# One more K-pair by seven products, and the evacuation of a PSUM bank as one ScalarE copy, in a four-layer transformer trunk

## The chip, the cores and the metric

The kernel runs on one core of one Trainium2 chip. The metric is the device time of one execution in microseconds, over everything the kernel does: loading the weights from HBM, all four sublayer pairs, and the store of the output. A core has TensorE (PE; its weight loads are listed apart as PEld), VectorE (DVE), ScalarE (ACT), GpSimd (POOL) and SyncE (SP), each with an instruction queue of its own, which works in order. TensorE writes to PSUM, of which the kernel uses eight banks of 512 fp32 columns.

## The reference, cut to what matters

Sequence length is 256, model width 2048, MLP width 8192, and there are four residual layers: a mixer and an MLP, twice (`DEPTH = 2`; the first mixer is latent attention with an mLSTM, the second dilated attention). The change touches the MLPs and the final norm alone:

```
def squared_relu_mlp(h, w1, w2):
    return jnp.square(jax.nn.relu(h @ w1)) @ w2

    for layer in range(DEPTH):
        i = layer // 2
        h = rms_norm(x, norm_mix[layer])
        ...
        x = x + mix
        x = x + squared_relu_mlp(rms_norm(x, norm_mlp[layer]), mlp_w1[layer], mlp_w2[layer])
    return rms_norm(x, norm_final)
```

`w1` is 2048 x 8192 and `w2` 8192 x 2048 in each of the two layers, in float32.

## The kernel before

**Three-pass products.** Every float32 operand is split in a high part in the format `FR` (float32r), in which it goes to TensorE, and the remainder (`hi`, `lo`; `xh`, `xl`). For a weight tile `wr` ScalarE writes the high part `wh` (line 135) and VectorE the remainder `wl` (line 136). A product is then three matmuls (`mm_three`, lines 154 to 156). In the first MLP product, which is made with features on the partitions, a matmul of 512 columns takes both parts of the tokens at once (line 164), and one of 256 columns adds the weight's remainder (line 168); the two halves of the PSUM bank must be added afterwards.

**The MLP.** The hidden width is worked in four quarters of 2048 features, 16 blocks of 128 each. A block `h` is 32 matmuls into one bank (bank 3 for all blocks but the first eight of a layer); its evacuation, `evac_h`, adds the two halves with `both` (lines 283 to 286): ScalarE copies the upper half of the bank to SBUF (`bt_h`), VectorE adds the lower half, still in PSUM, to it (`hu`). Then ScalarE applies Relu and Square. The next block can't start before both of these reads of the bank are done, since it writes the same bank.

**The second product** multiplies a quarter's 2048 hidden features, as eight pairs of 128-row K tiles, with `w2`, for two column ranges of 1024 one after the other ("first half" and "second half" of the quarter below). A pair is done in one of two ways. `steps_seven` does the 2 x 2 block product of a pair with seven block products rather than eight: 21 matmuls of 512 columns, in two steps of 9 (`go_a`) and 12 (`go_b`). It needs sums of weight tiles (`ta`, `tb`, lines 225 to 228), each split again in high part and remainder, and sums of the hidden tiles, made in `evac_h` (`hp`, then `pt`, lines 1039 to 1047). `eight` does it directly: 24 matmuls, two weight tiles of 128 x 1024, and hidden tiles `ht`. `SEVEN`, line 22, says how many of the eight pairs go by seven products, 5 here.

**Order.** `woven` puts the steps of the sevens between the blocks: in the first half of a quarter between its blocks 8 to 15, in the second half between blocks 0 to 7 of the next quarter. Then come the eights. After these VectorE adds the results to the residual `x` (`late_y`, line 1074; `early_y`, lines 1055 to 1065, after the sevens). The last quarter has no second half of this kind: in the first layer it has three sevens and five eights there, whatever `SEVEN` is, and in the second layer `finish` does those columns directly. The program's text is not the order on the engines: a scheduler orders each engine's queue at build time, and the rows in the section on the change show what it made.

**Buffers.** Raw weight tiles have 4 buffers, `wh` and `wl` 4 each, those of `ta` and `tb` 3 each. `hp` has two, `bt` two of 256 columns, `pt` has `SEVEN`, `ht` 2 x (8 - `SEVEN`).

Of the kernel before, what the change touches and what calls it, by code (L numbers as in the profile page):

```python
# [9 lines left out]
F32 = mybir.dt.float32  # L10
FR = mybir.dt.float32r
AF = mybir.ActivationFunctionType
OP = mybir.AluOpType

P = 128
S = 256
# [2 lines left out]
KD = D // P  # L19
FF = 8192  # L20
NQ = 4
SEVEN = 5
EPS = 1e-6
BIG = -3.0e38
MLA_SCALE = 192 ** -0.5
# [44 lines left out]
def trunk(ctx: ExitStack, tc: tile.TileContext, plan, a, c_first, c_even, c_odd, out):  # L70
    nc = tc.nc
# [23 lines left out]
    def acc(name, bank=None):  # L95

        if bank is None:
            bank = n_a[0] % 4
            n_a[0] += 1
        return pacc.tile([P, 512], F32, name=name, tag=f"acc{bank}", bufs=1)  # L100
# [181 lines left out]
    def both(pool, out, ac, name):  # L282

        t = pool.tile([P, S], F32, name=f"bt_{name}", tag="bt", bufs=2)
        nc.scalar.activation(t, ac[:, S:], AF.Copy)
        nc.vector.tensor_add(out, ac[:, :S], t)  # L286
# [664 lines left out]
    def finish(H, wq, evac_y, scale, sm):  # L951

        gfs = []
        for i in range(2):
            gfs.append(sm.tile([P, 1024], F32, name=f"gf{i}", tag="hp", bufs=2))
            nc.gpsimd.dma_start(gfs[i], a["norm_final"][i * 1024:(i + 1) * 1024]
                                .rearrange("(o d) -> o d", o=1).to_broadcast([P, 1024]))

        def gf(lo, hi):
            return gfs[lo // 1024][:, lo % 1024:(hi - 1) % 1024 + 1]  # L960

        ss = [sm.tile([P, 5], F32, name=f"ss_f{b}") for b in range(NB)]

        def stats(b, i, v):
            nc.scalar.activation(junk[:, :v.shape[-1]], v, AF.Square, accum_out=ss[b][:, i:i + 1])

        def gain(c):
            def go():
                for b in range(NB):
                    nc.vector.tensor_mul(x[b][c], x[b][c], gf(c * 512, (c + 1) * 512))  # L970
            return go

        for c in range(2):
            for b in range(NB):
                stats(b, c, x[b][c])
        weave(steps_tokens(Late(H), wq, 1024, 512, evac_y(2), name="y"), [gain(0), gain(1)])
        for b in range(NB):
            stats(b, 2, x[b][2])

        def add(b, o, ac):  # L980
            nc.vector.scalar_tensor_tensor(x[b][3][:, o:o + 256], ac[:, :256], scale["s"][:, b:b + 1],
                                           x[b][3][:, o:o + 256], OP.mult, OP.add)

        def evac_a(ac):
            for b in range(NB):
                add(b, 0, ac[b])
                stats(b, 3, x[b][3][:, 0:256])
                nc.vector.tensor_mul(x[b][3][:, 0:256], x[b][3][:, 0:256], gf(1536, 1792))

        weave(steps_tokens(Late(H), wq, 1536, 256, evac_a, kt=4, name="y"), [gain(2)])  # L990
        w = [weights(wq, k, 4, 1792, 256) for k in range(0, 16, 4)]
        for b in range(NB):
            ac = acc(f"z{b}")
            for k in range(16):
                hi, lo = (t[:, k % 4, :] for t in w[k // 4])
                mm_three(ac[:, :256], operand(H[k], b), (hi, lo), k == 0, k == 15)
            add(b, 256, ac)
            stats(b, 4, x[b][3][:, 256:])
            t = sm.tile([P, 3], F32, name=f"var_f{b}")
            nc.vector.tensor_reduce(t[:, 0:1], ss[b], mybir.AxisListType.X, OP.add)  # L1000
            nc.vector.tensor_scalar(t[:, 1:2], t[:, 0:1], 1.0 / D, EPS, OP.mult, OP.add)
            nc.gpsimd.tensor_tensor(t[:, 2:3], t[:, 1:2], neg_half[:, :1], OP.pow)
            r = t[:, 2:3]
            rows = slice(b * P, (b + 1) * P)
            for c in (0, 1):
                nc.vector.tensor_scalar(x[b][c], x[b][c], r, None, OP.mult)
                nc.sync.dma_start(out[0, rows, c * 512:(c + 1) * 512], x[b][c])
            nc.vector.scalar_tensor_tensor(x[b][3][:, 256:], x[b][3][:, 256:], r, gf(1792, 2048), OP.mult, OP.mult)
            nc.scalar.activation(x[b][2], x[b][2], AF.Copy, scale=r)
            nc.sync.dma_start(out[0, rows, 1024:1536], x[b][2])  # L1010
            nc.scalar.activation(x[b][3][:, 0:256], x[b][3][:, 0:256], AF.Copy, scale=r)
            nc.sync.dma_start(out[0, rows, 1536:2048], x[b][3])

    def mlp(layer, norm, nxt):
        st = ExitStack()
        sm = st.enter_context(tc.tile_pool(name=f"mlp{layer}", bufs=1))
# [4 lines left out]
        def evac_h(H):  # L1021
            def make(c):
                box = {}

                def go(f, ac):
                    u = sm.tile([P, S], F32, name="hu", tag="hu", bufs=2)
                    both(sm, u, ac, "h")
                    nc.scalar.activation(u, u, AF.Relu)  # L1028
                    if c >= SEVEN:
                        nc.scalar.activation(u, u, AF.Square)  # L1030
                        H[2 * c + f] = sm.tile([P, 2, S], FR, name="ht", tag="ht", bufs=2 * (NF // 2 - SEVEN))
                        split_to(H[2 * c + f], u)
                        return
                    if f == 0:
                        box["r"] = sm.tile([P, 8, P], F32, name="hp", tag="hp", bufs=2)
                    r = box["r"]
                    dst = r[:, 1:3, :] if f == 0 else r[:, 0:4:3, :]
                    v = u.rearrange("p (b t) -> p b t", b=NB)
                    nc.scalar.activation(dst, v, AF.Square)
                    if f == 1:  # L1040
                        nc.vector.tensor_tensor(r[:, 4:6, :], r[:, 1:3, :], r[:, 2:4, :], OP.subtract)
                        nc.vector.tensor_tensor(r[:, 6, :], r[:, 5, :], r[:, 1, :], OP.subtract)
                        nc.vector.tensor_tensor(r[:, 7, :], r[:, 0, :], r[:, 6, :], OP.add)
                        pt = sm.tile([P, 2, 8, P], FR, name="pt", tag="pt", bufs=SEVEN)
                        nc.scalar.activation(pt[:, 0], r, AF.Copy)
                        nc.vector.tensor_tensor(pt[:, 1], r, pt[:, 0].bitcast(F32), OP.subtract)
                        H[2 * c], H[2 * c + 1] = (pt, 0), (pt, 1)
                return go
            return make
# [56 lines left out]
        for q in range(NQ):  # L1106
            last = q == NQ - 1
            wq = ("mlp_w2", layer, q * (FF // NQ))
            seven, eight = steps_seven(sm, H, list(range(SEVEN)), wq, 0, early_y(0), late_y(0))
            woven(hs[NF // 2:], sum(seven, []))  # L1110
            run(*eight)
            if last and nxt is None:
                finish(H, wq, evac_y, scale, sm)
                break
            pairs = list(range(3 if last else SEVEN))
            seven, eight = steps_seven(sm, H, pairs, wq, 1024, early_y(2), late_y(2))
# [78 lines left out]
```

## Time and profile before

| | |
|---|---|
| median of 3 runs | 2154.32 us (2150.76 to 2155.19) |
| profiled execution | 2148.98 us, its span 2147.1 us |
| TensorE busy | 2116.2 us, 99% of the span |
| VectorE busy | 1667.3 us, 78% |
| ScalarE busy | 1249.1 us, 58% |
| granted TensorE clock, mean | 0.999 |
| moved by DMA | 404.51 MB, 188 GB/s |

The profiled execution is one run; 1.9 us of its time lie outside the span. A matmul's duration in the trace (about 390 ns for 512 columns) is longer than the distance to the next one's start, since matmuls overlap in the array: what TensorE can do is read from starts, and its busy share of 99% hides short stalls. Instructions on VectorE overlap a little too.

### The profile page before, as it was taken

What the parts mean: (1) busy time and instruction counts of PE and PEld (TensorE: products, weight loads), DVE (VectorE), ACT (ScalarE), POOL (GpSimd) and SP (SyncE); (2) the same over time, 40 slices, a digit from 0 to 9 for tenths busy, and PEclk for the clock granted to TensorE, in tenths of its full rate; (3) what the DMA queues carried; (4) which work ended last, traced back from release to release, by engine and by line L of the source; (5) the groups of instructions that cost most, each with busy time, mean ns of one, the idle gap of its engine ahead of it and who ended that gap; (6) DMA issues with size and microseconds to landing.
All of it is one profiled execution on the core that took longest, in us unless ns stands there. A gap on an engine that the chain in (4) does not pass through costs nothing. (4 is left out here: it accounts for less than half of the span.)

```text
span 2147.1 us, 29491 instructions
## 1 busy us (share of the span) xinstructions
PE 2116.2 (99%) x10995; PEld 1808.9 (84%) x10995; DVE 1667.3 (78%) x2346; ACT 1249.1 (58%) x1851; POOL 5.6 (0%) x12
## 2 busy tenths in 40 slices
PE   9999999999999999999999999999999999999998
PEld 8998888888888888888888888888888888888887
DVE  5678556878978888998877667557888889888975
ACT  6676445666665665666544544556656656566653
POOL 0000000000000000000000000000000000000000
PEclk9999999999999999999999999999999999999999
DMA  8554555555555555565555555455556556556664
GB/s 296 170 175 145 166 179 177 185 197 187 198 191 197 193 187 200 189 197 195 195 195 170 179 171 176 160 188 174 190 191 198 194 196 195 198 188 195 211 207 141
DMA packets 115279, 404.51 MB, mean 188 GB/s; under 512 B 12928, under 2 KB 13568, under 8 KB 115136
## 3 DMA queue, kind: packets, MB, share of 16 engines
q1 hardware_dynamic: 114624, 401.07, 56.7%
q8 instruction: 86, 1.41, 0.3%
q0 software_dynamic: 368, 1.51, 0.3%
q14 instruction: 57, 0.47, 0.1%
q10 hardware_dynamic: 144, 0.06, 0.0%
HBM read 400.49 MB, written 2.10 MB: 187 GB/s over the span
## 5 line engine op out<-in xcount | busy, mean ns | idle before, releaser
L136 DVE TENSOR_TENSOR wl<-wr,wh 128x1024 fp32r<-128x1024 f32 (+4 forms) x769 | 876.5, 1146 | 352.4 <-ACT wh L135 343.2
L135 ACT ACTIVATE wh<-wr 128x1024 fp32r<-128x1024 f32 (+4 forms) x769 | 763.2, 996 | 585.9 <-PE h L164 154.7
L164 PE MATMUL h<-T,wh 128*128 128x512 f32 x2048 | 518.1, 395 | 15.2 <-DVE hu L286 14.3
L164 PEld LDWEIGHTS h<-T,wh 128*128 128x128 f32 x2048 | 370.6, 188 | 107.4 <-DVE hu L286 37.3
L168 PEld LDWEIGHTS h<-T,wl 128*128 128x128 f32 x2048 | 279.2, 190 | 20.3
L168 PE MATMUL h<-T,wl 128*128 128x256 f32 x2048 | 285.3, 282 | 0.0
L154 PE MATMUL yc<-wh,ht 128*128 128x512 f32 x360 | 140.3, 390 | 0.0
L155 PE MATMUL yc<-wl,ht 128*128 128x512 f32 x360 | 140.2, 389 | 0.0
L156 PE MATMUL yc<-wh,ht 128*128 128x512 f32 x360 | 140.1, 389 | 0.0
L1028 ACT ACTIVATE hu<-hu 128x256 f32<-128x256 f32 x128 | 52.6, 415 | 109.8 <-DVE hu L286 109.8
L155 PE MATMUL ym<-wl,pt 128*128 128x512 f32 x292 | 114.5, 392 | 0.0
L154 PE MATMUL ym<-wh,pt 128*128 128x512 f32 x292 | 114.5, 392 | 0.0
L156 PE MATMUL ym<-wh,pt 128*128 128x512 f32 x292 | 113.6, 389 | 0.0
L225 DVE TENSOR_TENSOR ta<-wr,wr 128x1024 f32<-128x1024 f32 x73 | 89.2, 1222 | 30.6 <-DMA wr<-in_mlp_w 30.3
L154 PE MATMUL o<-wh,M 128*128 128x512 f32 x256 | 102.3, 399 | 0.0
L156 PE MATMUL o<-wh,M 128*128 128x512 f32 x256 | 99.8, 390 | 0.0
L155 PE MATMUL o<-wl,M 128*128 128x512 f32 x256 | 99.7, 389 | 0.0
L135 ACT ACTIVATE wh<-tb 128x1024 fp32r<-128x1024 f32 x73 | 76.9, 1053 | 35.5 <-DVE tb L228 35.2
L135 ACT ACTIVATE wh<-ta 128x1024 fp32r<-128x1024 f32 x73 | 77.0, 1055 | 30.4 <-DVE ta L225 30.2
L155 PE MATMUL yc<-wl,pt 128*128 128x512 f32 x235 | 91.8, 390 | 0.0
L154 PE MATMUL yc<-wh,pt 128*128 128x512 f32 x235 | 91.7, 390 | 0.0
L156 PE MATMUL yc<-wh,pt 128*128 128x512 f32 x235 | 91.6, 390 | 0.0
(314 smaller groups left out, 3343.0 us busy)
## 6 DMA issues: line engine op xcount, KB each, us to landing
wr<-in_mlp_w SPq DMA_DIRECT2D x512, 512.0 KB, 3.6
wr<-in_od_w_qkv SPq DMA_DIRECT2D x96, 512.0 KB, 4.2
wr<-in_ev_w_in SPq DMA_DIRECT2D x32, 512.0 KB, 3.5
wr<-in_ev_w_out SPq DMA_DIRECT2D x32, 512.0 KB, 3.4
wr<-in_od_w_out SPq DMA_DIRECT2D x32, 512.0 KB, 3.5
wr<-in_ev_w_in SPq DMA_DIRECT2D x24, 344.0 KB, 3.1
wr<-in_ev_w_in SPq DMA_DIRECT2D x15, 364.0 KB, 5.5
wr<-in_mla_w_ukv SPq DMA_DIRECT2D x8, 512.0 KB, 3.6
```

What stands on the lines that cost most here:

```text
L135: nc.scalar.activation(hi, raw, AF.Copy)
L136: nc.vector.tensor_tensor(lo, raw, hi.bitcast(F32), OP.subtract)
L154: nc.tensor.matmul(ac, xh, hi, start=first, stop=False)
L155: nc.tensor.matmul(ac, xh, lo, start=False, stop=False)
L156: nc.tensor.matmul(ac, xl, hi, start=False, stop=last)
L164: nc.tensor.matmul(acs[f], hi[:, j, f * P:(f + 1) * P], Ts[j].rearrange("p a t -> p (a t)"), start=first and j == 0, stop=False)
L168: nc.tensor.matmul(acs[f][:, :S], lo[:, j, f * P:(f + 1) * P], Ts[j][:, 0, :], start=False, stop=last and j == n - 1)
L225: nc.vector.tensor_tensor(ta, r0, r1[:, 0:1, :].to_broadcast([P, 2, 512]), OP.add)
L1028: nc.scalar.activation(u, u, AF.Relu)
```

## The change

`SEVEN` goes from 5 to 6, so one more pair in each half of a quarter is done by seven products; this applies to the first half of all quarters and to the second half of three quarters, in both layers. By `SEVEN`, `pt` gets six buffers and `ht` four. To make room, `hp` gets one buffer. The evacuation of a block no longer uses `both`: ScalarE copies the whole bank, 512 columns, to SBUF (now line 1027), and VectorE adds the two halves in SBUF (now line 1029). `bt` has two buffers of 512 columns. In `finish` the gains of the final norm are loaded in three pieces, into the buffers of `hp` and `bt`, not two.

```diff
-SEVEN = 5
+SEVEN = 6
...
-        for i in range(2):
-            gfs.append(sm.tile([P, 1024], F32, name=f"gf{i}", tag="hp", bufs=2))
-            nc.gpsimd.dma_start(gfs[i], a["norm_final"][i * 1024:(i + 1) * 1024]
-                                .rearrange("(o d) -> o d", o=1).to_broadcast([P, 1024]))
+        for i, (o, n, tag, bufs) in enumerate(((0, 1024, "hp", 1), (1024, 512, "bt", 2), (1536, 512, "bt", 2))):
+            g = sm.tile([P, n], F32, name=f"gf{i}", tag=tag, bufs=bufs)
+            nc.gpsimd.dma_start(g, a["norm_final"][o:o + n].rearrange("(o d) -> o d", o=1).to_broadcast([P, n]))
+            gfs.append((o, n, g))
...
                 def go(f, ac):
+                    t = sm.tile([P, 512], F32, name="bt_h", tag="bt", bufs=2)
+                    nc.scalar.activation(t, ac, AF.Copy)
                     u = sm.tile([P, S], F32, name="hu", tag="hu", bufs=2)
-                    both(sm, u, ac, "h")
+                    nc.vector.tensor_add(u, t[:, :S], t[:, S:])
                     nc.scalar.activation(u, u, AF.Relu)
...
-                        box["r"] = sm.tile([P, 8, P], F32, name="hp", tag="hp", bufs=2)
+                        box["r"] = sm.tile([P, 8, P], F32, name="hp", tag="hp", bufs=1)
```

ScalarE's queue at the start of a second half (first layer, blocks 0 and 1 of the second quarter), before; `wh` is a weight tile's high part, with `ta` or `tb` on the right where it is that of a sum, and `bt_h` the copy out of the bank:

```order
L135 ACTIVATE wh_4968<-wr_4966 128x1024
L285 ACTIVATE bt_h<-h_4857 128x256
L1028 ACTIVATE hu<-hu 128x256
L1039 ACTIVATE hp<-hu 128x256
L135 ACTIVATE wh_5015<-wr_5013 128x1024
L135 ACTIVATE wh_5037<-wr_5035 128x1024
L135 ACTIVATE wh_5075<-ta_5068 128x1024
L285 ACTIVATE bt_h<-h_4943 128x256
```

and now:

```order
L135 ACTIVATE wh_4979<-wr_4977 128x1024
L1027 ACTIVATE bt_h<-h_4868 128x512
L1030 ACTIVATE hu<-hu 128x256
L1041 ACTIVATE hp<-hu 128x256
L135 ACTIVATE wh_5029<-wr_5023 128x1024
L135 ACTIVATE wh_5034<-ta_5027 128x1024
L135 ACTIVATE wh_5044<-wr_5025 128x512
L1027 ACTIVATE bt_h<-h_4954 128x512
```

The copy stands where it stood and is of 512 columns; the weight tiles ahead of the second one are others, since a step of the next seven pair now comes in ahead of the third block.

VectorE's queue at the end of a second half, where the eights run out and the sevens of the next quarter begin (first layer), before; `x<-yc` are the four updates of the residual after the eights, `ta`, `tb` the sums of weight tiles for the first seven pair of the next half, `wl` remainders:

```order
L225 TENSOR_TENSOR ta_5609<-wr_5605,wr_5607 128x1024
L227 TENSOR_TENSOR tb_5610<-ta_5609,wr_5605 128x512
L136 TENSOR_TENSOR wl_5612<-wr_5605,wh_5611 128x1024
L136 TENSOR_TENSOR wl_5617<-ta_5609,wh_5616 128x1024
L228 TENSOR_TENSOR tb_5610<-tb_5610,wr_5607 128x512
L136 TENSOR_TENSOR wl_5627<-wr_5607,wh_5626 128x512
L1074 SCALAR_TENSOR_TENSOR x_75<-yc_4844,iv_mlp_3681,x_75 128x512
L1074 SCALAR_TENSOR_TENSOR x_79<-yc_4842,iv_mlp_3681,x_79 128x512
L136 TENSOR_TENSOR wl_5623<-tb_5610,wh_5622 128x1024
```

and now:

```order
L136 TENSOR_TENSOR wl_5633<-wr_5626,wh_5632 128x1024
L225 TENSOR_TENSOR ta_5630<-wr_5626,wr_5628 128x1024
L1048 TENSOR_TENSOR pt<-hp,pt 128x1024
L227 TENSOR_TENSOR tb_5631<-ta_5630,wr_5626 128x512
L1076 SCALAR_TENSOR_TENSOR x_75<-yc_4855,iv_mlp_3681,x_75 128x512
L1076 SCALAR_TENSOR_TENSOR x_79<-yc_4853,iv_mlp_3681,x_79 128x512
L136 TENSOR_TENSOR wl_5638<-ta_5630,wh_5637 128x1024
L1076 SCALAR_TENSOR_TENSOR x_76<-yc_4854,iv_mlp_3681,x_76 128x512
L1076 SCALAR_TENSOR_TENSOR x_80<-yc_5563,iv_mlp_3681,x_80 128x512
L228 TENSOR_TENSOR tb_5631<-tb_5631,wr_5628 128x512
L136 TENSOR_TENSOR wl_5648<-wr_5628,wh_5647 128x512
L136 TENSOR_TENSOR wl_5679<-wr_5676,wh_5678 128x1024
```

The conversions for the next half's first pair, which stood ahead of the four updates of `x`, now stand among and behind them, and the second sum `tb` (with its remainder, one row further on) waits behind all four.

## Rows read from the trace of the kernel before

**Rows 1.** The page: busy time (share of the span) of TensorE to ScalarE; granted clock.

```profile
PE 2116.2 (99%) x10995; PEld 1808.9 (84%) x10995; DVE 1667.3 (78%) x2346; ACT 1249.1 (58%) x1851; POOL 5.6 (0%) x12
...
PEclk9999999999999999999999999999999999999999
```

**Rows 2.** Waits: us in total, times, longest us.

```profile
ACT wh L135 <- PE h L164: 154.7, 124, 1.9
...
PEld h L164 <- DVE hu L286: 37.3, 55, 1.4
...
PE h L164 <- DVE hu L286: 14.3, 34, 1.0
```

**Rows 3.** Windows, blocks and products of both layers: us, busy us (instructions) by engine.

```profile
401.87:995.21 593.34, 585.23 (x2960) 491.93 (x2959) 508.24 (x615) 363.15 (x505) 0.00 (x0) 1.00 0.58 193
1485.95:2077.90 591.95, 584.87 (x2962) 492.27 (x2961) 509.31 (x615) 363.16 (x505) 1.11 (x2) 1.00 0.59 195
```

**Rows 4.** The same windows, instructions on the blocks' bank alone (no GpSimd column).

```profile
401.87:995.21 593.34, 324.17 (x1793) 280.49 (x1792) 23.71 (x57) 20.95 (x57) 1.00 0.58 193
1485.95:2077.90 591.95, 324.15 (x1794) 280.65 (x1792) 23.75 (x57) 20.97 (x57) 1.00 0.59 195
```

**Rows 5.** Timeline of TensorE, one block; then the eights' first matmul and its successor.

```profile
406.66 1.98 PE L164 MATMUL h<-T,wh 128*128 128x512 f32 x8
...
412.22 0.40 PE L154 MATMUL ym<-wh,pt 128*128 128x512 f32 x1
...
474.06 0.40 PE L154 MATMUL yc<-wh,ht 128*128 128x512 f32 x1
...
490.40 0.39 PE L154 MATMUL ym<-wh,pt 128*128 128x512 f32 x1
```

**Rows 6.** Timeline of all engines, one handing-over of the bank.

```profile
420.32 1.23 DVE L225 TENSOR_TENSOR ta<-wr,wr 128x1024 f32<-128x1024 f32 x1 [1.57 <-DMA wr<-in_mlp_w]
...
421.58 1.06 ACT L135 ACTIVATE wh<-ta 128x1024 fp32r<-128x1024 f32 x1 [1.29 <-DVE ta L225]
...
422.50 0.39 PE L156 MATMUL yc<-wh,pt 128*128 128x512 f32 x1
422.55 0.36 ACT L285 ACTIVATE bt_h<-h 128x256 f32<-128x256 f32 x1
423.33 0.42 DVE L286 TENSOR_TENSOR hu<-h,bt_h 128x256 f32<-128x256 f32 x1
...
423.80 0.50 PE L164 MATMUL h<-T,wh 128*128 128x512 f32 x1 [0.91 <-DVE hu L286]
```

**Rows 7.** Instructions by line and shape: busy us, mean ns | idle before.

```profile
L286 DVE TENSOR_TENSOR hu<-h,bt_h 128x256 f32<-128x256 f32 x128 | 52.8, 418 | 1.4 <-ACT bt_h L285 1.3
...
L285 ACT ACTIVATE bt_h<-h 128x256 f32<-128x256 f32 x128 | 46.5, 370 | 4.5 <-PE h L168 4.5
...
L301 DVE TENSOR_TENSOR ht<-hu,ht 128x256 fp32r<-128x256 f32 x48 | 20.1, 419 | 5.8 <-ACT ht L300 5.8
...
L1059 ACT ACTIVATE yp<-ym 128x512 f32<-128x512 f32 x15 | 9.0, 597 | 2.5 <-PE ym L156 2.5
```

**Rows 8.** Timeline of VectorE, conversions of one seven pair.

```profile
484.16 1.22 DVE L136 TENSOR_TENSOR wl<-wr,wh 128x1024 fp32r<-128x1024 f32 x1
485.30 1.22 DVE L136 TENSOR_TENSOR wl<-ta,wh 128x1024 fp32r<-128x1024 f32 x1
486.44 0.68 DVE L228 TENSOR_TENSOR tb<-tb,wr 128x512 f32<-128x512 f32 x1
487.04 0.68 DVE L136 TENSOR_TENSOR wl<-wr,wh 128x512 fp32r<-128x512 f32 x1
487.64 1.40 DVE L1074 SCALAR_TENSOR_TENSOR x<-yc,iv_mlp,x 128x512 f32<-128x512 f32 x2
```

**Rows 9.** Windows, two quarters of the first layer.

```profile
560.60:736.20 175.60, 172.39 (x868) 144.43 (x868) 149.80 (x181) 106.05 (x146) 0.00 (x0) 1.00 0.58 192
736.20:909.20 173.00, 171.67 (x868) 144.54 (x867) 150.00 (x182) 105.71 (x146) 0.00 (x0) 1.00 0.59 195
```

**Rows 10.** Instructions by line in 560.6 to 736.2, VectorE and ScalarE.

```profile
L136 DVE TENSOR_TENSOR wl<-wr,wh 128x1024 fp32r<-128x1024 f32 x54 | 65.6, 1220 | 16.3 <-ACT wh L135 15.2 <-ACT bt_h L285 0.8
L225 DVE TENSOR_TENSOR ta<-wr,wr 128x1024 f32<-128x1024 f32 x10 | 12.2, 1222 | 5.1 <-DMA wr<-in_mlp_w 5.1
...
L135 ACT ACTIVATE wh<-wr 128x1024 fp32r<-128x1024 f32 x55 | 58.0, 1055 | 36.1 <-PE h L164 19.0 <-PE yc L156 13.4 <-issue 2.2
```

More of the change, by code (lines that the diff above doesn't have):

```diff
@@ L953, in finish @@
         gfs = []
-        for i in range(2):
-            gfs.append(sm.tile([P, 1024], F32, name=f"gf{i}", tag="hp", bufs=2))
-            nc.gpsimd.dma_start(gfs[i], a["norm_final"][i * 1024:(i + 1) * 1024]
-                                .rearrange("(o d) -> o d", o=1).to_broadcast([P, 1024]))
+        for i, (o, n, tag, bufs) in enumerate(((0, 1024, "hp", 1), (1024, 512, "bt", 2), (1536, 512, "bt", 2))):
+            g = sm.tile([P, n], F32, name=f"gf{i}", tag=tag, bufs=bufs)
+            nc.gpsimd.dma_start(g, a["norm_final"][o:o + n].rearrange("(o d) -> o d", o=1).to_broadcast([P, n]))
+            gfs.append((o, n, g))
         def gf(lo, hi):
-            return gfs[lo // 1024][:, lo % 1024:(hi - 1) % 1024 + 1]
+            return next(g[:, lo - o:hi - o] for o, n, g in gfs if o <= lo < o + n)
         ss = [sm.tile([P, 5], F32, name=f"ss_f{b}") for b in range(NB)]
```

## The prediction

> **What bounds the kernel now.** I read the page first: TensorE is busy for 2116.2 of 2147.1 us, and its clock is fully granted in all slices [rows 1]. So this is a kernel bound by TensorE, and a change counts by the matmuls it removes and by the short stalls that the busy share hides. The list of waits says what stalls TensorE in the MLPs: one thing only, `hu`, VectorE's addition that empties the bank of a block, 34 times as a gap of the array and 55 times as a gap of the weight loads [rows 2]. Nothing there waits for a converted weight tile; it is ScalarE that waits for TensorE to give weight buffers back (154.7 us) [rows 2], so the conversions run ahead.
>
> The size of these stalls comes from starts. 72 matmuls of 512 columns of the eights take 490.40 − 474.06 = 16.34 us, 0.227 us each, and a block takes 412.22 − 406.66 = 5.56 us [rows 5]. The two windows hold 56 blocks each (1792 matmuls) and 2960 − 1793 = 1167 others [rows 3, 4]. At that pace a window would take 56 × 5.56 + 1167 × 0.227 = 576.3 us; they took 593.3 and 592.0 [rows 3]. The kernel thus loses 17.0 + 15.7 = 32.7 us at the handing-over of the bank.
>
> One handing-over shows how [rows 6]. The products between two blocks issue their last matmul at 422.50, and the next block could start at 422.73. But ScalarE was held by a weight tile's copy, which waited for `ta`, and began to read the bank at 422.55; VectorE was in another conversion and came to its addition at 423.33; the block started at 423.80, 1.07 us late. The bank is given back after two turns in two queues.
>
> **The change, part by part.** *Matmuls.* A pair by seven products has 21 matmuls for 24. The first half changes in 4 quarters of 2 layers, the second in 3 of 2: 14 pairs, 42 matmuls, 42 × 0.227 = 9.5 us less, all of it on TensorE's path [rows 5]. The weight bytes loaded are the same.
>
> *The evacuation.* The bank is now free after ScalarE's copy of 512 columns. The trace has the same copy out of PSUM: 0.597 us, for 0.370 of 256 columns [rows 7]. What goes is the 0.418 us addition and, above all, the time the addition stands behind a conversion of 1.2 us in VectorE's queue. In the example the bank would be free at 422.55 + 0.60 = 423.15 and the block start at 423.20, 0.47 us late in place of 1.07. That is one of the worst cases, because the copy itself was late; where it starts at once (as the order shows, it keeps its place in ScalarE's queue) the bank is free 0.65 us after the block's last matmul, and the shortest filling between two blocks, one step of 9 matmuls, lasts 9 × 0.227 = 2.0 us. A copy may thus start 1.3 us late and cost nothing. With one more pair 12 steps stand before 8 blocks, not 10, so four blocks of eight have two steps ahead of them, where two had. I expect nearly all of the 32.7 us back, and leave 3 us for late copies. Bounds: none left, or half of it (16 us) if ScalarE's queue is late as often as VectorE's was.
>
> [...]
>
> *ScalarE's load.* 128 copies longer by 0.227 us make 29 us; a seven pair has three and a half weight copies for two, 1.5 × 1.055 × 14 = 22 us [rows 10]. 1249 + 51 = 1300 us is 61% of the span; no bound.
>
> *VectorE's load*, which is the price. By starts a conversion of 1024 columns takes 1.14 us and one of 512 takes 0.60 [rows 8]. A seven pair has four of the first (three remainders, `ta`) and three of the second, 6.36 us, for the 2 × 1.14 = 2.28 of an eight: 4.1 us more. The sixth `pt` adds one more instruction of 1024 per quarter, about 1.2 us with the small additions set against the two `ht` that go. A quarter has 149.8 us of VectorE work now [rows 9], and will have 149.8 + 2 × 4.1 + 1.2 = 159.2. TensorE needs 16 × 5.56 + 354 × 0.227 = 169.3 us for a quarter now, and 1.4 less then: 167.9. VectorE goes from 88% to 95% of what TensorE needs, and has 8.7 us per quarter to wait in. Now it waits 175.6 − 149.8 = 25.8 us [rows 9], of which 15.2 for ScalarE's copies and 5.1 for a load of the next seven pair [rows 10]. The 15.2 are not its own fault: in the same stretch ScalarE waits 32.4 us for TensorE to free weight buffers [rows 10]. They shrink by themselves when VectorE has less lead. The 5.1 stay.
>
> The tight place is the end of the eights. These last 10.9 us (48 matmuls) where they lasted 16.3, and the order shows the conversions for the next pair sinking among and behind the four updates of `x`. Counted from the last block's end: addition possible at 0.65; then an eight's remainder, the `hp` sums, `wl`, `ta`, `pt`, `tb`, together some 6.3 us, to 6.9; the first update must wait for its bank, free 12 matmuls before the eights' end, at 8.2; then two updates at 0.7 [rows 8], a `wl` of 1.14, two updates (the last can't start before 10.9) to 12.1, `tb` 0.6, a half `wl` 0.6, a block's `wl` 1.14, the remainder of `tb` 1.14, to about 15.6. TensorE reaches that remainder after the eights, 17 products and the 4 matmuls of the next block that the scheduler put ahead: 10.9 + 21 × 0.227 = 15.7. It fits with nothing to spare. There are 13 such ends; I put 0.5 us on each, 7 us (bounds 0, and 1.5 us each or 20 in all).
>
> *`hp` with one buffer, `pt`, `ht`, the gains.* The Square that writes the next `hp` follows, through Relu, an addition that stands behind the old `pt` in VectorE's queue, so the wait is covered by that order; without that cover it would be one `pt` of 1.2 us, off TensorE's path. The gains are loaded when the buffers come free, before the last eights, and used after them; one more transfer on GpSimd's queue, which is idle. Nothing.
>
> *Sum*, against the profiled execution: −9.5 − 32.7 + 3 + 7 = −32.2 us, from 2148.98 to 2116.8. The median of the runs shown is 5.3 us above that execution, so in its measure 2154.3 − 32.2 = **2122 us**. Its own range is 2112 to 2130.
>
> **The rivals.** *VectorE turns half a bound:* the ends of the eights and the densest second halves cost 1.5 us each rather than 0.5, or copies come late behind weight copies that wait for `ta`, as in [rows 6]: 9 to 21 us more of the gain are lost, 2131 to 2143. For it: 95% load in queues that work in order. Against it: buffers of four tiles and a scheduler that places work around the gaps.
>
> *Only the products count:* the copy of the whole bank is as late as the addition was, and the 32.7 us stay; with the 9.5 and part of the 7, 2145 to 2152. For it: in [rows 6] ScalarE too was late. Against it: the margin of 1.3 us.
>
> *VectorE becomes the bound, and the kernel slower:* if it keeps its 25.8 us of waiting per quarter, a quarter takes 159.2 + 25.8 = 185.0 for 175.6. The two windows are 1185.3 / 174.3 = 6.8 quarters, so +64 us: 2218. It decides from the point where the waiting exceeds 175.6 − 159.2 = 16.4 us per quarter. Against it stands that most of that waiting ends with TensorE's own release of buffers.
>
> **How the numbers follow.** Forecast 57%, half a bound 23%, products only 11%, VectorE the bound (anywhere from 2155 up) 9%. The range of 8 in 10 runs from 2110 (nothing left of the stalls, no cost at the eights' ends) to 2143, the far end of the first rival. A difference under 0.2%, 4.3 us, can't be told from none. Faster: the first two cases and over half of the third, 0.87; same: the rest of it and a little of the last, 0.06; slower 0.07.
>
> **What would show it.** 10953 matmul records or so, 42 fewer. No wait of a block for `hu`, but for `bt_h`, under 5 us in all; `bt_h` near 600 ns; the addition still near 419 ns. VectorE busy for about 1735 us, ScalarE for 1300. The two windows from the first seven to the last block shorter by 14 to 18 us each. I am wrong if TensorE's waits in the MLPs name `wl` or `pt` with more than 15 us, or if blocks still start late by the bank.

## The result, and the profile after

The changed kernel takes 2126.83 us (median of 4 runs, 2125.58 to 2129.44), the kernel before 2153.6 in the same series; the ratio is 0.9879, with a 95% interval from 0.9862 to 0.9896. The prediction was 2122 (2110 to 2143): the direction came true, and the wait that the change was to remove is gone, but the gain is 5 us smaller. The profiled executions differ by 2148.98 − 2125.81 = 23.2 us, where the sum had said 32.2; the one of the kernel before is 4.6 us faster than the median of its series, the one of the changed kernel 1.0.

The page of the changed kernel, busy time and share of the span (2124.0 us), against [rows 1]:

```profile
PE 2098.3 (99%) x10953; PEld 1803.9 (85%) x10953; DVE 1727.1 (81%) x2432; ACT 1301.9 (61%) x1871; POOL 6.1 (0%) x13
```

TensorE has its 42 matmuls less. VectorE (1735 had been worked out) and ScalarE (1300) have the load that was counted. The list of waits of the changed kernel (us in total, times, longest us), against [rows 2]:

```profile
DVE wl L136 <- ACT wh L135: 268.2, 265, 2.9
ACT wh L135 <- PE h L164: 121.0, 110, 1.7
ACT hu L1030 <- DVE hu L1029: 106.3, 104, 1.9
...
ACT wh L135 <- DVE ta L225: 63.1, 55, 4.3
...
DVE ta L225 <- DMA wr<-in_mlp_w: 46.0, 40, 2.7
...
PEld h L164 <- ACT wh L135: 11.6, 9, 1.8
...
PE h L164 <- ACT wh L135: 7.8, 9, 1.4
...
PEld h L164 <- ACT bt_h L1027: 6.6, 11, 0.9
...
PE h L164 <- ACT bt_h L1027: 1.9, 6, 0.4
...
PEld ym L155 <- DVE wl L136: 1.0, 5, 0.2
```

TensorE's wait for the addition `hu` is gone. In its place the copy `bt_h` is late at times, and, which was not there before, a block at times waits for a converted weight tile `wh`. ScalarE waits less for TensorE (121.0 us, not 154.7): the conversions run less far ahead. The new lines that empty the bank, by line and shape (busy us, mean ns), against [rows 7]:

```profile
L1027 ACT ACTIVATE bt_h<-h 128x512 f32<-128x512 f32 x128 | 73.8, 583 | 6.1 <-PE h L168 6.1
L1029 DVE TENSOR_TENSOR hu<-bt_h 128x256 f32<-128x256 f32 x128 | 53.0, 419 | 2.3 <-ACT bt_h L1027 2.2
```

Both durations are near the forecast (597 and 419 ns). The addition does not get shorter by reading SBUF alone (419 ns, 418 before); only its place changed. (The row for two SBUF operands in [rows 7] is a subtraction of the same shape; here the addition itself shows it.) The windows of both layers' blocks and products, and of two quarters of the first layer, against [rows 3, 9] (us, then busy us and instructions by engine):

```profile
402.27:987.81 585.54, 580.83 (x2963) 493.86 (x2962) 541.00 (x660) 390.29 (x517) 0.00 (x0) 1.00 0.60 196
1473.13:2059.67 586.54, 581.37 (x2964) 493.66 (x2963) 540.72 (x660) 389.78 (x517) 1.12 (x2) 1.00 0.61 197
```

```profile
562.56:733.18 170.62, 169.19 (x862) 143.66 (x862) 158.19 (x193) 113.01 (x149) 0.00 (x0) 1.00 0.60 198
733.18:903.35 170.17, 168.96 (x862) 143.83 (x862) 158.22 (x193) 112.93 (x149) 0.00 (x0) 1.00 0.61 198
```

A quarter's VectorE work is 158.2 us (forecast 159.2), and a quarter takes 170.4 where TensorE's pace is 167.9. The two windows became only 7.8 and 5.4 us shorter, because more of the products now stand before a layer's last block: there are three and two matmuls more in them, not 21 fewer in each. They must be compared with their pace, as in the prediction: they were 32.5 us over it before, and are 8.6 + 9.6 = 18.2 us over it now. Together with the products, 9.5 + (32.5 − 18.2) = 23.8 us, near the 23.2 of the profiled executions. This number, the time of the two windows over the pace, is called the *lost time* below. It is taken from one execution of each kernel; the four of the changed kernel lie 4 us apart, so 2 or 3 us of it decide nothing.

Not all lost time is stalls. A *late start* is a matmul that starts over 0.15 us later than usual after its predecessor, counted from the starts in the trace. The kernel before has 45 late starts in the two windows, 22.4 us in all, and 43 of them are blocks that wait for `hu`. The changed kernel has 19, 13.0 us in all: nine blocks wait for `wh` (9.2 us) and nine for `bt_h` (3.6 us). The second matmul of a late block is often late too, by under 0.15 us: 6.0 us in all before, 1.5 now. Some 4 us more, in both kernels, lie in distances that exceed the pace by under 0.015 us each: the pace, worked out from one block and one row of products, is a little short, and this part of the lost time stays in both.

One late start shows where it comes from. The timeline of the changed kernel, VectorE, in the second half of the second quarter:

```profile
540.74 1.23 DVE L225 TENSOR_TENSOR ta<-wr,wr 128x1024 f32<-128x1024 f32 x1 [1.01 <-DMA wr<-in_mlp_w]
...
545.61 1.22 DVE L136 TENSOR_TENSOR wl<-tb,wh 128x1024 fp32r<-128x1024 f32 x1
546.74 0.42 DVE L1029 TENSOR_TENSOR hu<-bt_h 128x256 f32<-128x256 f32 x1
```

The same stretch on ScalarE:

```profile
542.00 1.06 ACT L135 ACTIVATE wh<-ta 128x1024 fp32r<-128x1024 f32 x1 [1.56 <-DVE ta L225]
543.45 1.06 ACT L135 ACTIVATE wh<-tb 128x1024 fp32r<-128x1024 f32 x1 [0.39 <-DVE tb L228]
544.42 0.62 ACT L135 ACTIVATE wh<-wr 128x512 fp32r<-128x512 f32 x1
544.94 0.58 ACT L1027 ACTIVATE bt_h<-h 128x512 f32<-128x512 f32 x1
547.19 0.42 ACT L1030 ACTIVATE hu<-hu 128x256 f32<-128x256 f32 x1 [1.67 <-DVE hu L1029]
547.52 1.04 ACT L135 ACTIVATE wh<-wr 128x1024 fp32r<-128x1024 f32 x1
```

And TensorE:

```profile
542.72 0.40 PE L154 MATMUL ym<-wh,pt 128*128 128x512 f32 x1
...
547.28 0.39 PE L156 MATMUL ym<-wh,pt 128*128 128x512 f32 x1
548.61 1.65 PE L164 MATMUL h<-T,wh 128*128 128x512 f32 x6 [0.94 <-ACT wh L135]
```

`ta` waits 1.0 us at the head of VectorE's queue for its raw tiles, `wh<-ta` 1.6 us at the head of ScalarE's for `ta`; the copy of the bank, whose block ended at 542.72, starts at 544.94. The addition comes at 546.74 behind conversions; the Relu waits for it at the head of ScalarE's queue, and behind the Relu stands the weight tile of the next block, which starts 1.1 us late. The bank no longer waits for VectorE, but ScalarE's queue does. All nine late `wh` come at such a place: two steps, 21 products, stand ahead of the block, and on ScalarE the block's `wh` follows right behind that Relu. Ahead of eight of them ScalarE stands for 1.67 or 1.68 us for `hu`; ahead of the ninth it stands for 1.53 us for `tb`.

### The profile page after: what moved, and what is told of

Same layout as the page of the kernel before. It is cut to its first block, busy times and chain, and to the rows that moved or that the text cites. A ratio compares the mean times of both kernels' runs of the same rounds, so it can differ in the third digit from the quotient of the medians.

```text
span 2124.0 us, 29506 instructions
## 1 busy us (share of the span) xinstructions
PE 2098.3 (99%) x10953; PEld 1803.9 (85%) x10953; DVE 1727.1 (81%) x2432; ACT 1301.9 (61%) x1871; POOL 6.1 (0%) x13
## 4 chain that ended last, share of the span: by engine, by line
PE 67%; DVE 19%; DMA 8%; issue 3%; ACT 2%; DVEq 0%; POOLq 0%; POOL 0%; SPq 0%; ACTq 0%
PE h L164 12%; DVE wl L136 11%; DMA wr<-in_mlp_w 8%; PE h L168 6%; PE k L164 3%; PE o L154 3%; PE o L156 3%; PE o L155 3%; PE q L164 3%; PE yc L154 3%; PE yc L155 3%; PE yc L156 3%; DVE ta L225 2%; PE v L154 2%; PE v L156 2%
## 5 line engine op out<-in xcount | busy, mean ns | idle before, releaser
L136 DVE TENSOR_TENSOR wl<-wr,wh 128x1024 fp32r<-128x1024 f32 (+4 forms) x769 | 865.8, 1136 | 270.4 <-ACT wh L135 264.9
L135 ACT ACTIVATE wh<-wr 128x1024 fp32r<-128x1024 f32 (+4 forms) x769 | 752.7, 987 | 512.9 <-PE h L164 121.0
L225 DVE TENSOR_TENSOR ta<-wr,wr 128x1024 f32<-128x1024 f32 x87 | 106.3, 1222 | 46.4 <-DMA wr<-in_mlp_w 46.0
L155 PE MATMUL ym<-wl,pt 128*128 128x512 f32 x348 | 136.7, 393 | 0.0
L156 PE MATMUL ym<-wh,pt 128*128 128x512 f32 x348 | 135.4, 389 | 0.0
L154 PE MATMUL ym<-wh,pt 128*128 128x512 f32 x348 | 135.4, 392 | 0.0
L135 ACT ACTIVATE wh<-ta 128x1024 fp32r<-128x1024 f32 x87 | 92.1, 1059 | 61.4 <-DVE ta L225 60.1
L135 ACT ACTIVATE wh<-tb 128x1024 fp32r<-128x1024 f32 x87 | 91.8, 1056 | 34.2 <-DVE tb L228 34.2
L154 PE MATMUL yc<-wh,pt 128*128 128x512 f32 x285 | 111.3, 390 | 0.0
L155 PE MATMUL yc<-wl,pt 128*128 128x512 f32 x285 | 111.2, 390 | 0.0
L156 PE MATMUL yc<-wh,pt 128*128 128x512 f32 x285 | 110.9, 389 | 0.0
L136 DVE TENSOR_TENSOR wl<-tb,wh 128x1024 fp32r<-128x1024 f32 x87 | 106.1, 1220 | 3.8 <-ACT wh L135 3.3
L136 DVE TENSOR_TENSOR wl<-ta,wh 128x1024 fp32r<-128x1024 f32 x87 | 106.0, 1218 | 0.0
L154 PE MATMUL yc<-wh,ht 128*128 128x512 f32 x240 | 93.6, 390 | 0.0
```

Of the source, the lines that this page charges most:

```text
L135: nc.scalar.activation(hi, raw, AF.Copy)
L136: nc.vector.tensor_tensor(lo, raw, hi.bitcast(F32), OP.subtract)
L154: nc.tensor.matmul(ac, xh, hi, start=first, stop=False)
L155: nc.tensor.matmul(ac, xh, lo, start=False, stop=False)
L156: nc.tensor.matmul(ac, xl, hi, start=False, stop=last)
L225: nc.vector.tensor_tensor(ta, r0, r1[:, 0:1, :].to_broadcast([P, 2, 512]), OP.add)
```

## The experiments

All are compared with the kernel before, run on the same chip in the same series.

**The parts apart.** Copy alone: the changed kernel with `SEVEN = 5` (so also with one buffer for `hp` and the gains in three pieces).

> The whole-bank copy alone: SEVEN stays 5, everything else as in the changed kernel. Theory A (each part has its own effect; the 18 us of stalls that the changed kernel keeps come from VectorE's and ScalarE's queues being full with the sixth pair's conversions): nearly all of the 32.7 us of stalls go, no product is saved, so 2153.6 - 28 = 2124 to 2130 us, and waits of a block for a weight tile are under 3 us. Rival B (the copy leaves half the stalls by itself, whatever VectorE's load is): 2136 to 2140 us, with the same late weight tiles as in the changed kernel.

Measured 2128.0 us, ratio 0.9888 [0.9875, 0.9902]. Its windows:

```profile
402.59:983.15 580.56, 579.88 (x2962) 493.57 (x2961) 507.12 (x616) 374.52 (x505) 0.00 (x0) 1.00 0.57 197
1473.75:2056.58 582.83, 580.34 (x2961) 493.25 (x2960) 506.59 (x615) 374.54 (x505) 1.12 (x2) 1.00 0.57 197
```

The lost time falls from 32.5 to 10.7 us, and by the ratios the copy brings 24 of the change's 26 us. The 2 us between them lie inside the two intervals: that the sixth pair gains anything on top of the copy is not shown. 11 starts are late, by 4.9 us in all, and nine of them (4.6 us) wait for the copy; no block waits for `wh`:

```profile
PEld h L164 <- ACT bt_h L1027: 9.7, 18, 1.7
```

The sixth pair alone, with the old way of emptying the bank:

```diff
-                    nc.scalar.activation(t, ac, AF.Copy)
+                    nc.scalar.activation(t[:, :S], ac[:, S:], AF.Copy)
-                    nc.vector.tensor_add(u, t[:, :S], t[:, S:])
+                    nc.vector.tensor_add(u, ac[:, :S], t[:, :S])
```

> The sixth pair alone: SEVEN is 6, a block is evacuated as before (a copy of 256 columns by ScalarE, an addition by VectorE that reads the other half from PSUM). Theory A: the 9.5 us of matmuls go, and VectorE's fuller queue makes the addition later, so the stalls grow by about as much: 2145 to 2155 us, stalls at the bank over 33 us. Rival B (the parts are independent): 2153.6 - 9.5 = 2144 us, stalls at the bank of 33 us as before.

Measured 2131.22 us, 0.9904 [0.9889, 0.9919]: faster than either theory allowed. The blocks still wait for `hu`, but a third as often as in [rows 2], and longer each time:

```profile
PE h L164 <- DVE hu L1029: 14.5, 11, 2.2
```

Lost time 27.2 us: besides the 9.5 us of matmuls, the sixth pair takes away 5 us of the old stalls in this execution, the slowest of its five (2135.79), and some 11 us by the ratio. That two steps now stand before four blocks of eight fits this, but is not tested apart. The parts do not add up (24 and 21 us alone, 26 together): both remove the same stalls, and on top of the copy the sixth pair *adds* 18.2 − 10.7 = 7.5 us of lost time to the 9.5 it saves. In late starts it adds 13.0 − 4.9 = 8.1 us: the late `wh` come in with 9.2 us, while the late copies fall from 4.6 to 3.6.

**Where the 18 us come from.** First theory: the raw tiles come late. One more buffer for them (`r1` of a seven pair in a buffer of its own; to make room `ta` has one, not two):

```diff
-                r1 = load(w, [(2 * k, c + 512, 512), (2 * k + 1, c, 512)], (2, 512))
+                r1 = load(w, [(2 * k, c + 512, 512), (2 * k + 1, c, 512)], (2, 512), pool, 1)
-                ta = pool.tile([P, 2, 512], F32, name=f"ta{n_w[0]}", tag="ta", bufs=2)
+                ta = pool.tile([P, 2, 512], F32, name=f"ta{n_w[0]}", tag="ta", bufs=1)
```

> The changed kernel with one more raw weight buffer in the MLPs, used for the second tile of a seven pair; the space comes from the sums ta, which have one buffer, not two. In the changed kernel VectorE waits 46 us for the loads of ta, and ScalarE 63 us for ta. Theory A1 (the late stalls begin with the load of the next seven pair): these waits fall by half and 5 to 10 us of time go, 2117 to 2122 us. Rival A2 (they begin with the addition hu standing in VectorE's queue, on which Relu waits in ScalarE's queue): no change, 2125 to 2129 us; with a single ta buffer even up to 2135.

Measured 2128.81 us, 0.9891 [0.9877, 0.9905]; lost time 20.2. No gain; the single `ta` may have eaten one, so this is inconclusive.

Second theory: ScalarE's queue is held by the Relu that waits for the addition. If so, a slower addition, which the bank does not wait for, must cost much:

```diff
-                    nc.vector.tensor_add(u, t[:, :S], t[:, S:])
+                    nc.gpsimd.tensor_tensor(u, t[:, :S], t[:, S:], OP.add)
```

> The changed kernel with the addition of the bank's two halves on GpSimd, which is idle, in place of VectorE; it reads SBUF alone. Theory A2 (the addition waits behind conversions in VectorE's queue, Relu waits for it in ScalarE's queue, and the next weight copies and bank copies wait behind Relu): ScalarE's 106 us of waiting for hu become the addition's own time, the late weight tiles go, 5 to 10 us less: 2117 to 2122 us. Rival A1 (the load of the next seven pair is what is late): the same time as the changed kernel, 2125 to 2129 us. If GpSimd needs over 2 us for an addition or slows VectorE, slower than 2129.

Measured 2202.27 us, 1.023 [1.0216, 1.0244], lost time 93.9. GpSimd's addition, and what ScalarE and TensorE wait for:

```profile
L1029 POOL TENSOR_TENSOR hu<-bt_h 128x256 f32<-128x256 f32 x128 | 223.0, 1745 | 1791.5 <-ACT bt_h L1027 1791.5
```

```profile
ACT hu L1030 <- POOL hu L1029: 212.7, 108, 3.2
...
PEld h L164 <- ACT wh L135: 45.5, 26, 3.0
PE h L164 <- ACT wh L135: 34.1, 18, 2.6
```

1.33 us more per addition doubles ScalarE's wait, and the weight tiles behind it come late: this chain can cost a lot when it is lengthened. But the edit does more than that. Beside GpSimd's additions 43 instructions of VectorE take longer, 23 us in all (in 562 to 734 us the remainders `wl` of 512 columns take 783 ns in the mean, 683 in the changed kernel), and in the two windows TensorE runs for 27 us at a granted clock of 0.50 (0.99 in the mean of each window), which makes, as an estimate, some 14 of the 93.9 us. So it does not follow that the chain makes the 18 us, and the next runs shorten it. Relu and Square in one VectorE instruction behind the addition, so that ScalarE waits for neither:

```diff
-                    nc.scalar.activation(u, u, AF.Relu)
...
-                    nc.scalar.activation(dst, v, AF.Square)
+                    nc.vector.scalar_tensor_tensor(dst, v, 0.0, v, OP.max, OP.mult)
```

> The changed kernel, with Relu and Square done by one VectorE instruction (the maximum with 0, times the sum itself) behind the addition, so that ScalarE's queue never stands behind VectorE's addition. VectorE gets 16 x about 0.42 = 6.7 us more per quarter, 158.2 + 6.7 = 165 of the 167.9 that TensorE needs. Theory (what is left of the stalls comes from ScalarE's queue held by the Relu that waits for the addition, which delays the next weight tiles and copies): the wait of 106.3 us for hu goes, the late wh and bt_h go, stalls 18.2 to 6 or so, about 2116; if the 98% load of VectorE then binds in places, up to 2125. Rival (the stalls come from VectorE's load itself, the conversions being late whatever ScalarE does): more load makes more stalls, 30 us or more, 2138 and above.

> As the kernel with Relu and Square on VectorE, but with five pairs by seven products, so VectorE's load is about 150 + 6.7 = 157 us per quarter, as in the changed kernel. Theory (ScalarE's queue held by the Relu): of the 10.7 us of stalls that the copy alone leaves some 3 stay, the time goes from 2128 to about 2120. Rival (VectorE's load): with the load of the changed kernel come its stalls, some 18 us, 2135.

Measured 2134.22 us (0.9908 [0.9895, 0.9922]) with six pairs, 2136.62 (0.992 [0.9906, 0.9933]) with five; lost time 25.4 and 19.1. Of ScalarE's 106 us of waiting for `hu` 19 stay, ahead of `ht`, and TensorE waits more for the copy, less for `wh`. Six pairs:

```profile
PEld h L164 <- ACT bt_h L1027: 20.2, 18, 2.0
...
PE h L164 <- ACT bt_h L1027: 12.4, 17, 1.5
...
PEld h L164 <- ACT wh L135: 3.4, 8, 0.5
```

The theory of the held Relu comes true for the weight tiles: with six pairs the late starts for `wh` fall from 9.2 to 0.4 us. But those for the copy grow from 3.6 to 15.4, and the kernel gets slower, so what the theory promised, the 18 us back, does not come. The four largest of them stand behind a `wh<-ta` that waited 4.2 to 4.4 us for `ta` on VectorE, which has the work now. The rival of VectorE's load forecast both times within 4 us. The sixth pair in the first halves only, alone and with the former edit:

```diff
-            pairs = list(range(3 if last else SEVEN))
+            pairs = list(range(3 if last else 5))
```

> The changed kernel, but with six pairs by seven products in the first halves of the quarters only and five in the second halves. Against before 8 x 3 = 24 matmuls go, 5.4 us, where the change removes 42, 9.5 us. Theory (the loss of the sixth pair sits in the second halves, where the steps are densest and late weight tiles are seen): the stalls of the two layers fall from 18.2 us to about 11, as with the copy alone (10.7), and TensorE no longer waits for a late wh; against the changed kernel +4.1 - 7 = -3 us, about 2124. Rival (the loss comes with the load of VectorE over the whole quarter, wherever the pair is): stalls of 14 to 15, which is +4.1 - 4 = 0, about 2127.

> Both edits: six pairs by seven products in the first halves and five in the second, Relu and Square on VectorE. Theory of ScalarE's queue: stalls of about 4 us, 24 matmuls fewer than before: about 2116 to 2118, the fastest of these. Rival of VectorE's load: some 20 us of stalls, 2133.

Measured 2133.21 us (0.9904 [0.989, 0.9917]) and 2140.24 (0.9938 [0.9925, 0.9952]), lost time 23.7 and 29.1. Both miss. The first has less work on VectorE than the changed kernel (1705.5 us busy, not 1727.1) and does not lose less: 5.5 us more in this execution, the slowest of its four, and some 1 us more by the ratios, which is inside the noise. So the loss is not a matter of the second halves, nor of the load alone. Its late `wh`, eight with 8.9 us, now stand in the first halves, one in each quarter, where the sixth pair is.

Load by itself: the copy alone (five pairs), and on VectorE each addition once more into a tile that nobody reads.

```diff
                     nc.vector.tensor_add(u, t[:, :S], t[:, S:])
+                    d = sm.tile([P, S], F32, name="dummy", tag="dummy", bufs=1)
+                    nc.vector.tensor_add(d, t[:, :S], t[:, S:])
```

> The copy of the whole bank with five pairs by seven products, and on VectorE behind each addition the same addition once more into a tile that nothing reads. Nothing waits for it; VectorE gets 16 x 0.42 = 6.7 us more per quarter, as much as Relu and Square gave it in the kernel with five pairs and those on VectorE, while ScalarE's work stays as with the copy alone. Theory (load: the stalls grow with VectorE's work, wherever it comes from): stalls from 10.7 to about 18 us, time from 2128 to about 2135, VectorE busy about 1717 us. Rival (the stalls of the kernels with Relu on VectorE came from their new chain, the square standing behind conversions, not from the load): stalls of 10 to 12, 2128 to 2129.

Measured 2149.95 us, 0.9993 [0.998, 1.0006], VectorE busy 1698.9, lost time 29.1: 128 additions of 0.42 us that no engine waits for take away the whole gain. Late are the copies again (15.7 us) and some `wl` (5.8 us); but the order on VectorE changed with the edit, so this is not the load by itself either. The next two edits are meant to take load off VectorE. First, half of each `pt` remainder on GpSimd:

```diff
-                        nc.vector.tensor_tensor(pt[:, 1], r, pt[:, 0].bitcast(F32), OP.subtract)
+                        nc.gpsimd.tensor_tensor(pt[:, 1, :4], r[:, :4], pt[:, 0, :4].bitcast(F32), OP.subtract)
+                        nc.vector.tensor_tensor(pt[:, 1, 4:], r[:, 4:], pt[:, 0, 4:].bitcast(F32), OP.subtract)
```

> The changed kernel, with half of each remainder of pt (512 of 1024 columns, needed only blocks later) made by GpSimd. VectorE loses 48 x 0.54 = 26 us in all, 3.2 per quarter, from 158.2 to 155; no step that TensorE or ScalarE soon waits for is moved to GpSimd. Theory of the load: stalls from 18.2 to 14 or so, 2122 to 2124. Rival (the stalls of the changed kernel are given by the order of its steps, in which two steps stand before more of the blocks, not by the load): 18 us as before, 2126 to 2128; and if the GpSimd work of about 3.5 us each holds a tile that ScalarE waits for, above that.

Measured 2145.5 us, 0.9962 [0.9948, 0.9976], lost time 37.4; ScalarE waits for GpSimd's part only 5.8 us in all. But VectorE is busy for 1728.8 us, not less than in the changed kernel: its other instructions take longer (the remainders `wl` 1154 ns in the mean, not 1136, `ta` 1248, not 1222; the last section has rows), and that eats the 26 us that were taken off it. So this run is no test of less load. Second, the addition left out:

```diff
-                    nc.vector.tensor_add(u, t[:, :S], t[:, S:])
-                    nc.scalar.activation(u, u, AF.Relu)
+                    nc.scalar.activation(u, t[:, :S], AF.Relu)
```

> The changed kernel without VectorE's addition of the two halves of the bank (the second half is left out of the result); ScalarE copies the bank and applies Relu to the copy. VectorE loses 6.7 us per quarter, 158.2 to 151.5, and ScalarE no longer waits for VectorE there. Theory of the load, and that of ScalarE's queue too: stalls from 18.2 to under 8, 2114 to 2117, which bounds what any other way of adding the halves could win. Rival (what is left comes from late raw tiles and from the order of the steps): stalls of 14 or more, 2122 and above.

Measured 2143.18 us, 0.9952 [0.9935, 0.997]; lost time 34.2. VectorE has 41 us less to do, ScalarE does not wait for it after a block, and the kernel is 16 us slower than with the addition. Its waits, against those of the changed kernel above:

```profile
ACT wh L135 <- DVE ta L225: 144.6, 71, 6.1
...
DVE ta L225 <- DMA wr<-in_mlp_w: 106.7, 71, 3.5
...
PEld ym L155 <- DVE wl L136: 17.1, 27, 1.5
```

VectorE now stands at `ta` for loads that have not landed, twice as long as in the changed kernel, and ScalarE for `ta`; what is queued behind comes late. That fits the rival of that run (raw tiles and order), which does not say why the loads are late. The edits of these last three runs also make the scheduler put VectorE's instructions in another order (TensorE's hardly changes, SyncE's not at all): when the two orders are laid side by side, 764 of 2304 stand elsewhere with the addition left out, 507 of 2218 with the extra one (the additions `hu` themselves not counted). The last run changes the order and hardly the load: the extra addition of 2 columns, not 256.

```diff
+                    d = sm.tile([P, 2], F32, name="dummy", tag="dummy", bufs=1)
+                    nc.vector.tensor_add(d, t[:, :2], t[:, S:S + 2])
```

> The same as the kernel with the extra addition (five pairs, whole-bank copy), but the extra addition is of 2 columns, not 256: VectorE gets the same 128 instructions more and hardly any time, so its load stays near that of the copy alone, while the scheduler again puts VectorE's instructions in another order (some 320 of 2292 stand elsewhere than with the copy alone; TensorE's and SyncE's orders are the same). Theory (the order of VectorE's and ScalarE's queues decides how much of the stalls is left, and any edit redraws it): stalls clearly above the 10.7 us of the copy alone, 17 or more, 2135 us and above. Rival (the load decides, and the order does not matter): stalls of 10 to 13, 2128 to 2131.

Measured 2138.0 us, 0.9938 [0.9923, 0.9954], lost time 19.4: by the numbers, the theory of the order. But the trace says otherwise. Only 4 starts are late, by 4.0 us in all (11 and 4.9 with the copy alone). The rest is a slower pace; TensorE, eights of the first layer:

```profile
484.04 0.40 PE L156 MATMUL yc<-wh,ht 128*128 128x512 f32 x1
...
488.24 0.40 PE L156 MATMUL yc<-wh,ht 128*128 128x512 f32 x1
```

18 distances in 4.20 us are 0.233 us each, where [rows 5] have 0.227. Over the two windows this kernel is 1172.16 − 1163.39 = 8.8 us longer than the copy alone, all of it pace. So another order by itself brought no stalls here, though it changed less of the order than the extra addition of 256 columns did (236 of 2218, not 507), and the run is spoiled as a test of the time.

**What is shown and what stays open.** That the copy frees the bank and gains 24 us is shown. That the sixth pair then loses most of what it saves to late weight tiles is shown by the late starts: each stands behind a wait of ScalarE for VectorE, at one place in the order, and nearly all of them go when Relu leaves ScalarE. How to keep what the pair saves is not settled, nor is why the stalls of the other kernels are as large as they are. They are not the Relu's wait alone (taken away: more), not VectorE's load alone (with less of it: more), and the order was not changed by itself in a way that brought stalls. Every edit of the work also changed the order, so load and order were not told apart. No kernel here beat the changed one.

## Why the prediction was nearly right, by its steps

- *Matmuls, −9.5 us:* 42 fewer at an unchanged pace; right.
- *The bank's stalls, −32.7 us:* the wait for `hu` is gone, and the mechanism was right. The size was some 4 us too large: it took all time over the pace for the bank's, and that part is the pace itself, which stays in both kernels.
- *"Leave 3 us for late copies":* near: 3.6 us of late starts wait for the copy in the changed kernel, 4.6 with the copy alone. What blocks the copy was right too (it had been seen in [rows 6]: ScalarE held by `wh<-ta`).
- *7 us for VectorE's load:* the step that failed. It was put at the eights' ends, on the remainders `wl`; TensorE's weight loads wait for those only 1.0 us in all. What came is 9.2 us of late `wh` at blocks inside the halves, which the sum has at nothing: "the conversions run ahead" was read from the kernel before and no longer holds where two steps stand ahead of a block. `ta` waiting for its load, 5.1 us in [rows 10], was counted as VectorE's idle time and not as a hold on ScalarE. That 9.2 is near 7 is luck. These three terms account for most of the way from the 10 us of lost time that the sum left to the 18.2 measured.
- *The sixth pair without the copy* was taken to be worth its matmuls alone; it also removed 5 us of stalls or more, which the copy removes anyway.
- *The signs.* That the two windows would be 14 to 18 us shorter each was badly chosen: the work inside them changed. "If blocks still start late by the bank" came true in small: the waits for `bt_h` are 6.6 us on the weight loads and 1.9 on the array, where under 5 in all were expected.
- *Rivals:* the products alone (2145 to 2152) and VectorE as the bound (2218) did not come. "VectorE turns half a bound" named copies late behind `wh<-ta`, of which there are a few; 2126.8 lies below that case (2131 to 2143) and inside the forecast's own range (2112 to 2130).
- *The addition itself* takes 419 ns with both operands in SBUF, 418 with one in PSUM: the copy makes it no faster. The 24 us come from the bank being free earlier.

## What to carry to other kernels

When a PSUM bank is handed over through two queues, it can pay to let the first engine take all of it (here 24 us): price the gain by the time the second stands behind other work, not by its instruction (0.42 us here). A Relu that waited 1.67 us at the head of ScalarE's queue held the weight tile behind it here, and through that TensorE, whose block started 1.1 us late; count such waits into the copies and weight tiles behind. An edit that takes work off such a queue can make the kernel slower (here by 16 us); it also changed the order (764 of 2304 instructions), so measure it, and keep the edits apart. Run each part of a change alone: here one part brought nearly all of the gain.

## What the runs showed of the hardware

*The granted clock after a pause.* Where the slow addition on GpSimd let TensorE stand for 2.6 us, it came back at a granted clock of 0.50 in one place and of 1.00 in another. TensorE in that kernel, then stretches by windows (the column before the last two is the granted clock):

```profile
464.88 0.39 PE L156 MATMUL ym<-wh,pt 128*128 128x512 f32 x1
467.86 3.78 PE L164 MATMUL h<-T,wh 128*128 128x512 f32 x8 [2.59 <-ACT wh L135]
...
649.39 2.12 PE L164 MATMUL h<-T,wh 128*128 128x512 f32 x8 [2.58 <-ACT wh L135]
```

```profile
467.90:472.00 4.10, 4.10 (x11) 3.33 (x12) 2.97 (x3) 1.66 (x3) 0.00 (x0) 0.50 0.61 214
472.00:480.00 8.00, 8.00 (x39) 6.94 (x38) 3.83 (x5) 3.65 (x7) 1.28 (x1) 0.87 0.50 168
...
649.30:653.00 3.70, 3.61 (x20) 3.14 (x21) 3.39 (x4) 2.52 (x4) 0.00 (x0) 1.00 0.59 208
```

It is 0.50 in 467.9 to 472, after an idle time of 2.59 us; after one of 2.58 us it is 1.00. In the changed kernel, whose longest late start is 1.6 us, it is 1.00 in the mean of each window; but with the sixth pair alone it is 0.73 in 454.8 to 458.0, after an idle time of 2.01 us. So the length of one wait alone does not tell whether it falls. Where it was 0.50, the block's first eight matmuls take 3.78 us, 1.98 in [rows 5]; by the 4.1 us at 0.50 that stall cost, as an estimate, some 2 us more than itself.

*Instructions of GpSimd and VectorE took longer side by side.* GpSimd's addition of 128x256 takes 0.73 us in the 12 cases in which no instruction of VectorE runs beside it, up to 3.10 us beside VectorE's conversions, and 1.745 in the mean of all 128. The same kernel:

```profile
484.58 3.49 DVE L136 TENSOR_TENSOR wl<-wr,wh 128x1024 fp32r<-128x1024 f32 x3
...
485.56 3.10 POOL L1029 TENSOR_TENSOR hu<-bt_h 128x256 f32<-128x256 f32 x1 [7.03 <-ACT bt_h L1027]
...
614.25 0.73 POOL L1029 TENSOR_TENSOR hu<-bt_h 128x256 f32<-128x256 f32 x1 [9.57 <-ACT bt_h L1027]
```

VectorE pays too. With half of `pt` on GpSimd, a conversion that takes 1.22 us in [rows 10], where GpSimd does nothing, took 1.99:

```profile
777.99 1.75 POOL L1048 TENSOR_TENSOR pt<-hp,pt 128x512 fp32r<-128x512 f32 x1 [33.61 <-ACT pt L1047]
...
778.83 1.99 DVE L136 TENSOR_TENSOR wl<-wr,wh 128x1024 fp32r<-128x1024 f32 x1 [0.25 <-ACT wh L135]
```

So work put on an idle GpSimd did not take load off VectorE here (1728.8 us busy, 1727.1 in the changed kernel).

*A slower pace, its cause open.* In the kernel with the addition of 2 columns the MLPs' products from `ht` are 0.233 us apart, not 0.227, and the matmuls from `pt` take 392 to 395 ns, in the kernel with the extra addition of 256 columns 389 to 393; in the mixers the matmuls of `o` take 389 to 399 ns in both. TensorE's instructions and their order are the same as with the copy alone. The edit's new tile is of 8 bytes on each partition. With the tile of 256 columns the matmuls from `ht` take 389 to 390 ns, as in the changed kernel, with that of 2 columns 395 to 396. What makes the pace slower is not shown.
